# A hybrid decoder block with a product-key expert mixer: which token blocks are gathered, which are multiplied densely, and what runs on GpSimd

## The chip, the core and the metric

The kernel runs on one core of one Trainium2 chip. The metric is the device time of one execution in microseconds (us). Engines are named as in the profile: PE (TensorE matmuls), DVE (VectorE), ACT (ScalarE), POOL (GpSimd), SP (SyncE, which here only issues DMAs).

## The reference

The input is one sequence of 1024 tokens with 1024 features, in float32. After two attention-like mixers and a residual, each token goes through a mixer of 16384 single-neuron experts. Cut to what the change touches:

```
h2 = modulate(x, norm2_g, shift2, scale2)
q  = h2 @ w_q                                # 8 heads x 256
s1, s2 = q halves against 128 keys each      # 8 heads
# top 16 of each, then top 16 of the 256 sums -> 8*16 = 128 experts per token
experts = e1 * 128 + e2 ;  gates = softmax(scores)
a   = gelu(<h2[t], u_tab[experts[t, e]]>)    # 128 dot products of 1024 per token
out = sum_e gates[t, e] * a[t, e] * v_tab[experts[t, e]]
x   = rms_norm(x + gate2 * out, final_g)
```

## The kernel before, in words

The tokens stand in 8 blocks of 128. A **prelude** is run for each group of four blocks (512 tokens): norm, projections, gated linear attention, window attention, second norm, and the choice of the 128 experts of each token. Then comes the expert mixer, which is done in one of two ways.

**Gathered blocks** (blocks 0, 6 and 7). For each of the 128 chosen slots j, POOL issues an indirect DMA that fetches for each of the 128 tokens its own row of `peer_u` (a tile `u` of 128x1024, 512 KB; L605). DVE multiplies it with the tokens' rows `h2s` and sums (L610, which also leaves a short read of the accumulator). Every eighth slot is multiplied on POOL instead (L607) and summed on ACT (L608). When all 128 sums of a block are there, they go through gelu, and 128 rows of `peer_v` are gathered in the same way (L623) and added up with their weights on DVE (L625, tile `yacc`). All gathered tiles share six buffers of the pool `gp` (tag "g"), and so does `h2l`, the load from which PE transposes a gathered block's rows into `h2s`: a gather waits until the multiply that uses its buffer's last tile is done.

**Dense blocks** (blocks 1 to 5, DT = 640 tokens). All 16384 experts are multiplied, as 128 tiles of 128 experts, and the gates of experts that were not chosen are zero. Float32 matmuls are made of three passes each (L165 to L167) on tiles split in a high and a low part (ACT makes the high part, DVE subtracts: `uh` L696, `vl` L723, `wl` L718).
- `dense_u`: the tile's product with the 640 tokens, in two halves of 320 columns (8 x 3 matmuls each), then gelu into `ga`.
- `build_gates`: for each four tokens, two one-hot tiles (`o1` 4 x 128x128 on DVE L671; `o2` 128x512 on POOL L661 and ACT, one of four on DVE L659) go through PE (L672) and give the gates as a table, which is stored to DRAM (`gd`).
- `dense_w`: `gl = gd * ga` on POOL (L715), then its split `wl`.
- `dense_v`: for groups of VG = 3 tiles, 10 outputs of 128x512 (5 blocks x 2 halves) get 3 x 3 matmuls each. Three outputs stay in PSUM throughout (`keep`); the other seven are added to `acc` in SBUF on DVE (L741).

While the gates are built (no `dense_w` can run yet), 60 of the 128 tiles have their first product done ahead (`AHEAD`), 12 of them before the gates begin (`N1`). Their `ga` goes to DRAM (`gad`, issued by POOL) and comes back later. The dense blocks' transposed tokens `h2T` are loaded from DRAM after the second prelude (`load_h2T`).

The order of the instructions on each engine is decided when the program is built, by a scheduler that follows the code's priorities; on the chip each engine takes its instructions strictly in that order. The first 72 slots (`NU`) of block 0 are written before `build_gates`, its others and its `peer_v` rows after the first `o1`.

Of the kernel before, what the change touches and what calls it, by code (L numbers as in the profile page):

```python
# [41 lines left out]
def hymba_peer_kernel(ctx, tc, x, c, w_adaT, b_adaT, g1T, g2T, w_in, w_alpha, b_alphaT,  # L42
# [545 lines left out]
    def token_rows(blk, pool):  # L588
        g, b = divmod(blk, GB)
        h2 = gp.tile([128, 8, 128], F, name="h2l", tag="g")  # L590
        GP.dma_start(h2, h2d[g][:, :, b * 128:b * 128 + 128].rearrange("k p t -> p k t"))
# [6 lines left out]
        return h2s, sm.tile([128, 128], F, name="acts", tag="acts", bufs=1)  # L598

    def gather_u(blk, sel, work, j0=0, j1=128):  # L600
        exi, gates = sel
# [11 lines left out]
        wg = sm.tile([128, 128], F, name="wts", tag="wts", bufs=2)
        A.activation(wg, a, AF.Gelu)
        V.tensor_tensor(wg, wg, gates, AL.mult)
        return wg
# [32 lines left out]
    def build_gates(lists):  # L649
        """gd[b][i2][i1][t] = the sum of the gates of token t for expert (i1, i2)"""  # L650
        for b in range(ND):
            st = gt.tile([128, 128, 128], F, name="st", tag="st", bufs=1)
            for t0 in range(0, 128, 4):
# [4 lines left out]
                if t0 % 16 == 0:  # L658
                    V.tensor_tensor(o2, bc(iota.unsqueeze(1), [128, 4, 128]), e2, AL.is_equal)  # L659
                else:  # L660
                    GP.tensor_tensor(o2, bc(iota.unsqueeze(1), [128, 4, 128]), e2, AL.subtract)  # L661
                    A.activation(o2, o2, AF.Abs)
                    A.activation(o2, o2, AF.Relu, bias=1.0, scale=-1.0)
                for t in range(4):
                    e1, gate = (lists[:, n, b, t0 + t:t0 + t + 1] for n in (0, 2))
                    if t == 3 and t0 % 16 == 0:
                        A.activation(o1[:, t], iota, AF.Abs, bias=e1, scale=-1.0)
                        A.activation(o1[:, t], o1[:, t], AF.Relu, bias=1.0, scale=-1.0)
                        A.activation(o1[:, t], o1[:, t], AF.Copy, scale=gate)
                    else:  # L670
                        first.append(V.tensor_scalar(out=o1[:, t], in0=iota, scalar1=e1, scalar2=gate, op0=AL.is_equal, op1=AL.mult))  # L671
# [8 lines left out]
    def load_h2T():  # L680
        h2T = hx.tile([128, 2, 8, DT], R, name="h2T", tag="hT")
        n0 = GT - D0 * 128
        for k in range(8):
            raw = h2T[:, 1, k].bitcast(F)
            SP.dma_start(raw[:, :n0], h2d[0][k][:, D0 * 128:])
            SP.dma_start(raw[:, n0:], h2d[1][k][:, :DT - n0])
            A.activation(h2T[:, 0, k], raw, AF.Copy)
            GP.tensor_tensor(h2T[:, 1, k], raw, h2T[:, 0, k], AL.subtract)
        return h2T
# [186 lines left out]
```

## Time and profile before

| what | value |
|---|---|
| median of three runs | 3136.61 us (3133.43 to 3137.14) |
| span of the profiled execution | 3135.7 us, 0.9 us under that median |
| PE busy | 2808.3 us (90%) |
| DVE busy | 2747.9 us (88%) |
| POOL busy | 1982.1 us (63%) |
| ACT busy | 1169.0 us (37%) |
| moved by DMA | 767.16 MB, of these 427.61 MB issued by POOL |

Busy is the time in which an instruction of the engine runs, including the time that an instruction needs longer because another engine holds what it needs. Waiting is not busy. The shares are averages over stages that differ much, so the span is looked at in stages below.

### The profile page before, as it was taken

How to read it: one execution, taken by the hardware profiler on the slowest of the kernel's cores; microseconds unless marked ns; L12 is line 12 of the kernel's file. 1: busy time of each engine (PE TensorE's matmuls, PEld its weight loads, DVE VectorE, ACT ScalarE, POOL GpSimd, SP SyncE). 2: the span in 40 equal slices, each digit the busy share in tenths (PEclk: the TensorE clock that was granted, in tenths of full speed). 3: DMA queues.
4: the chain of work that ended last, by engine and by line, in shares of the span. 5: the costliest groups of instructions: out<-in, count | busy, mean ns of one | idle time of the engine just before them, and what ended most of it. 6: DMA issues, size and time to landing. Idle time of an engine off the chain costs nothing. (4 is left out here: it accounts for less than half of the span.)

```text
span 3135.7 us, 45458 instructions
## 1 busy us (share of the span) xinstructions
PE 2808.3 (90%) x15951; PEld 2487.2 (79%) x15951; DVE 2747.9 (88%) x4922; ACT 1169.0 (37%) x2181; POOL 1982.1 (63%) x1679
## 2 busy tenths in 40 slices
PE   5899978888888888888887999999999999999997
PEld 4698766767778877878787888888888887888886
DVE  7754699996599998898895899999999898999998
ACT  4444633343523454565462322222222322322222
POOL 2322565885454775554554688787777788877774
PEclk8999989967999999999998999999999999999998
DMA  8404312565522576757759899999999898999995
GB/s 315 164 29 132 124 55 96 196 224 168 169 68 95 191 244 251 285 184 295 267 193 378 291 309 318 323 311 342 345 334 339 289 333 306 322 317 333 335 333 182
DMA packets 296677, 767.16 MB, mean 245 GB/s; under 512 B 26992, under 2 KB 115328, under 8 KB 293888
## 3 DMA queue, kind: packets, MB, share of 16 engines
q0 software_dynamic: 116832, 427.61, 39.2%
q1 hardware_dynamic: 176736, 294.70, 27.7%
q10 hardware_dynamic: 2880, 41.94, 3.3%
q8 instruction: 125, 2.05, 0.3%
q14 instruction: 104, 0.85, 0.1%
HBM read 689.96 MB, written 74.71 MB: 244 GB/s over the span
## 5 line engine op out<-in xcount | busy, mean ns | idle before, releaser
L623 POOL DMA_INDIRECT v<-in_peer_v_dram,exi x384 | 523.2, 1363 | 354.9 <-DVE yacc L625 183.9
L167 PE MATMUL da<-h2T,uh 128*128 128x320 f32 x2048 | 649.1, 317 | 43.7 <-DVE uh L696 43.7
L165 PE MATMUL da<-h2T,uh 128*128 128x320 f32 x2048 | 649.5, 317 | 13.7 <-ACT ga L702 7.8
L605 POOL DMA_INDIRECT u<-in_peer_u_dram,exi x384 | 546.2, 1422 | 169.3 <-DVE acts L610 71.8
L166 PE MATMUL da<-h2T,uh 128*128 128x320 f32 x2048 | 647.0, 316 | 0.0
L625 DVE SCALAR_TENSOR_TENSOR yacc<-v,wts,yacc 128x1024 f32<-128x1024 f32 x381 | 537.3, 1410 | 29.1 <-DMA v<-in_peer_v_dram,exi 25.1
L610 DVE CUSTOM_DVE_ANT_0 u<-u,h2s 128x1024 f32<-128x1024 f32 x336 | 497.1, 1500 | 20.8 <-DMA u<-in_peer_u_dram,exi 19.2
L167 PEld LDWEIGHTS da<-h2T,uh 128*128 128x128 f32 x2048 | 395.9, 193 | 58.0 <-DVE uh L696 48.7
L165 PEld LDWEIGHTS da<-h2T,uh 128*128 128x128 f32 x2048 | 396.8, 194 | 26.6 <-ACT ga L702 10.4
L166 PEld LDWEIGHTS da<-h2T,uh 128*128 128x128 f32 x2048 | 396.4, 194 | 9.7
L165 PE MATMUL dv<-vl,wl 128*128 128x512 f32 x896 | 358.1, 400 | 29.3 <-DVE acc L741 25.1
L166 PE MATMUL dv<-vl,wl 128*128 128x512 f32 x896 | 352.9, 394 | 0.2 <-DVE vl L723 0.2
L167 PE MATMUL dv<-vl,wl 128*128 128x512 f32 x896 | 352.8, 394 | 0.0
L671 DVE TENSOR_SCALAR o<-iota,lists 128x128 f32<-128x128 f32 x600 | 320.7, 603 | 5.6 <-PE gt L672 5.6
L702 ACT ACTIVATE ga<-da 128x320 f32<-128x320 f32 x256 | 108.7, 430 | 467.9 <-PE da L167 374.5
L157 POOL TENSOR_TENSOR whl<-wraw,whl 128x512 fp32r<-128x512 f32 x104 | 147.1, 1419 | 209.5 <-ACT whl L156 199.3
L672 PE MATMUL gt<-o,o 128*128 128x128 f32 x1280 | 183.8, 291 | 68.6 <-DVE o L671 37.7
L715 POOL TENSOR_TENSOR gl<-gl,ga 128x640 f32<-128x640 f32 x128 | 218.0, 1704 | 23.7 <-issue 12.2
L672 PEld LDWEIGHTS gt<-o,o 128*128 128x128 f32 x1280 | 166.6, 200 | 83.6 <-DVE o L671 36.2
L696 DVE TENSOR_TENSOR uh<-ur,uh 128x1024 fp32r<-128x1024 f32 x128 | 185.2, 1447 | 45.1 <-ACT uh L695 45.0
L165 PEld LDWEIGHTS dv<-vl,wl 128*128 128x128 f32 x896 | 169.3, 189 | 68.7 <-DVE acc L741 35.3
L717 ACT ACTIVATE wl<-gl 128x640 fp32r<-128x640 f32 x128 | 94.3, 737 | 339.6 <-POOL gl L715 222.4
(264 smaller groups left out, 6176.7 us busy)
## 6 DMA issues: line engine op xcount, KB each, us to landing
ur<-in_peer_uT_dram SPq DMA_DIRECT2D x128, 512.0 KB, 6.3
vr<-in_peer_v_dram SPq DMA_DIRECT2D x128, 512.0 KB, 6.9
gd<-st ACTq DMA_DIRECT2D x20, 2048.0 KB, 19.9
gl<-gd SPq DMA_DIRECT2D x128, 320.0 KB, 7.0
wada<-in_w_adaT_dram SPq DMA_DIRECT2D x48, 512.0 KB, 5.4
wraw<-in_w_in_dram SPq DMA_DIRECT2D x80, 256.0 KB, 3.0
gad<-ga POOLq DMA_DIRECT2D x60, 320.0 KB, 4.8
ga<-gad SPq DMA_DIRECT2D x60, 320.0 KB, 4.7
```

The costliest lines, as they stand in the source:

```text
L157: (GP if kq % 2 or (not busy[0] and src is w_q) else V).tensor_tensor(hl[:, 1], raw, hl[:, 0], AL.subtract)
L165: PE.matmul(p, lhsT=lh[0], rhs=rh[0], start=first, stop=False)
L166: PE.matmul(p, lhsT=lh[0], rhs=rh[1], start=False, stop=False)
L167: PE.matmul(p, lhsT=lh[1], rhs=rh[0], start=False, stop=last)
L605: GP.indirect_dma_start(out=u, out_offset=None, in_=peer_u, in_offset=bass.IndirectOffsetOnAxis(ap=exi[:, j:j + 1], axis=0))
L610: V.tensor_tensor_reduce(out=u, in0=u, in1=h2s, scale=1.0, scalar=0.0, op0=AL.mult, op1=AL.add, accum_out=a[:, j:j + 1])
L623: GP.indirect_dma_start(out=v, out_offset=None, in_=peer_v, in_offset=bass.IndirectOffsetOnAxis(ap=exi[:, j:j + 1], axis=0))
L625: V.scalar_tensor_tensor(out=y, in0=v, scalar=wg[:, j:j + 1], in1=y, op0=AL.mult, op1=AL.add)
L671: first.append(V.tensor_scalar(out=o1[:, t], in0=iota, scalar1=e1, scalar2=gate, op0=AL.is_equal, op1=AL.mult))
L672: PE.matmul(p[:, t * 128:t * 128 + 128], lhsT=o2[:, t], rhs=o1[:, t], start=True, stop=True)
L696: V.tensor_tensor(hl[:, 1], u, hl[:, 0], AL.subtract)
L715: GP.tensor_tensor(g, g, ga, AL.mult)
```

## The change

- Blocks 0 to 3 (the first prelude's group) are gathered, blocks 4 to 7 (the second prelude's) are dense: DT goes from 640 to 512, one matmul of 512 columns in place of two of 320, 8 dense outputs in place of 10 (5 in `acc` in place of 7). There are 512 `u` and 512 `v` gathers in place of 384 and 384.
- `h2T` stays in SBUF from the second prelude; `load_h2T` is gone.
- All `u` multiplies are on DVE (L606 of the changed kernel), as are `gl = gd * ga` (L694) and all `o1` (L661). Half of the `o2` are on DVE (L654) and half on ACT alone (L657, L658). POOL keeps the gathers and the preludes' work.
- 40 tiles are done ahead in place of 60, 4 of them before the gates; the DMA that stores `ga` is issued by ACT.
- All `u` gathers of blocks 0 to 2 are written before `build_gates`, those of block 3 after the ahead tiles; all `v` gathers come after, with the dense tiles.

```diff
-D0 = 1
-ND = 5
+D0 = 4
+ND = 4
...
-    NU = 72
+    NU = 3
...
-            if j % 8 == 7:
-                GP.tensor_tensor(u, u, h2s, AL.mult)
-                A.activation(u, u, AF.Copy, accum_out=a[:, j:j + 1])
-            else:
-                V.tensor_tensor_reduce(out=u, in0=u, in1=h2s, scale=1.0, scalar=0.0, op0=AL.mult, op1=AL.add, accum_out=a[:, j:j + 1])
+            V.tensor_tensor_reduce(out=u, in0=u, in1=h2s, scale=1.0, scalar=0.0, op0=AL.mult, op1=AL.add, accum_out=a[:, j:j + 1])
...
-                if t0 % 16 == 0:
+                if t0 % 8 == 0:
                     V.tensor_tensor(o2, bc(iota.unsqueeze(1), [128, 4, 128]), e2, AL.is_equal)
                 else:
-                    GP.tensor_tensor(o2, bc(iota.unsqueeze(1), [128, 4, 128]), e2, AL.subtract)
-                    A.activation(o2, o2, AF.Abs)
+                    for t in range(4):
+                        A.activation(o2[:, t], iota, AF.Abs, bias=lists[:, 1, b, t0 + t:t0 + t + 1], scale=-1.0)
                     A.activation(o2, o2, AF.Relu, bias=1.0, scale=-1.0)
...
-        GP.tensor_tensor(g, g, ga, AL.mult)
+        V.tensor_tensor(g, g, ga, AL.mult)
...
-    N1 = 12
-    NX = 46
-    ORDER = (0, 7, 1, 2, 8, 3, 4, 9, 5, 6)
-    AHEAD = {i: n for n, i in enumerate(range(1, 120, 2))}
+    N1 = 4
+    ORDER = (0, 5, 1, 2, 6, 3, 4, 7)
+    AHEAD = {i: n for n, i in enumerate(range(1, 120, 3))}
...
-            GP.dma_start(gad[AHEAD[i]], ga)
+            A.dma_start(gad[AHEAD[i]], ga)
...
-        with tc.high_priority(offset=600):
-            h2T = load_h2T()
         for i in tiles[:N1]:
             ahead(i)
         decode(GB, NB)
-        gather_u(0, sels[0], work0, 0, NU)
+        wgs = [gather_u(0, sels[0], work0)]
+        for b in range(1, NU):
+            wgs.append(gather_u(b, sels[b], token_rows(b, sm)))
...
         build_gates(lists)
-        with tc.issue_after(first[0].ins):
-            y0 = gather_v(0, sels[0], gather_u(0, sels[0], work0, NU), sm)
         for n, i in enumerate(tiles[N1:]):
-            ahead(i, ux if n < NX and n % 2 == 1 else None)
+            ahead(i, ux if n % 2 == 1 else None)
+        with tc.issue_after(first[0].ins):
+            for b in range(NU, D0):
+                wgs.append(gather_u(b, sels[b], token_rows(b, sm)))
...
-    finish([y0], 0, GP)
-    for b in range(D0 + ND, NB):
-        finish([gather_v(b, sels[b], gather_u(b, sels[b], token_rows(b, sm)), sm)], b, GP)
+    for b in range(D0):
+        finish([gather_v(b, sels[b], wgs[b], sm)], b, GP)
```

Three places of the built order are needed below. The first is POOL. Before, its last work in the second prelude reads as follows (`whl` is a weight split of the prelude, `swr`, `grr` and `e` are small work of its norms and attention, xN counts equal rows):

```order
L605 DMA u<-in_peer_u_dram,exi 128x1024 x5
L305 TENSOR_TENSOR e<-e,kg 128x512
L605 DMA u<-in_peer_u_dram,exi 128x1024 x2
L607 TENSOR_TENSOR u<-u,h2s 128x1024
L605 DMA u<-in_peer_u_dram,exi 128x1024 x8
L607 TENSOR_TENSOR u<-u,h2s 128x1024
L605 DMA u<-in_peer_u_dram,exi 128x1024 x3
L147 TENSOR_TENSOR swr<-swv,mhalf 128x1
```

In the changed kernel the same stretch reads as follows (`h2l`, L591, is the load of the rows of the next gathered block, here block 1):

```order
L605 DMA u<-in_peer_u_dram,exi 128x1024 x5
L305 TENSOR_TENSOR e<-e,kg 128x512
L605 DMA u<-in_peer_u_dram,exi 128x1024 x19
L147 TENSOR_TENSOR swr<-swv,mhalf 128x1
L605 DMA u<-in_peer_u_dram,exi 128x1024 x24
L147 TENSOR_TENSOR swr<-swv,mhalf 128x1
L605 DMA u<-in_peer_u_dram,exi 128x1024
L445 TENSOR_TENSOR grr<-gss,mhalf 128x4
L605 DMA u<-in_peer_u_dram,exi 128x1024 x3
L591 DMA h2l<-h2d 128x8x128
```

More gathers stand ahead of the prelude's small work: over the whole second prelude 133 (block 0 and five of block 1) in place of 72, and no L607 in place of nine. After the prelude POOL's order is this, with only the small work of three finishes between the `v` gathers that follow:

```order
L605 DMA u<-in_peer_u_dram,exi 128x1024 x123
L591 DMA h2l<-h2d 128x8x128
L605 DMA u<-in_peer_u_dram,exi 128x1024 x128
L591 DMA h2l<-h2d 128x8x128
L605 DMA u<-in_peer_u_dram,exi 128x1024 x128
L618 DMA v<-in_peer_v_dram,exi 128x1024 x128
```

The `h2l` of block 2 stands behind the last 123 gathers of block 1.

The second place is PE, where the gates begin (`gt` is their PSUM tile, `dl` the transposes of the last expert lists, `h2p` the transposes of a gathered block's rows, `da` an ahead tile). Before:

```order
L165 MATMUL da<-h2T,uh 128x320
L672 MATMUL gt<-o_10167,o_10168 128x128 x3
L166 MATMUL da<-h2T,uh 128x320
L672 MATMUL gt<-o_10167,o_10168 128x128
L167 MATMUL da<-h2T,uh 128x320
```

Changed:

```order
L596 MATMUL h2p<-ident,h2l 128x128 x8
L584 MATMUL dl<-ident,ee 128x128
L584 MATMUL dl<-ident,gates 128x128
L596 MATMUL h2p<-ident,h2l 128x128 x8
L662 MATMUL gt<-o_10487,o_10488 128x128 x4
L662 MATMUL gt<-o_10500,o_10501 128x128 x4
L165 MATMUL da<-h2T,uh 128x512
```

The first eight `h2p` are those of block 1, the second eight those of block 2; the second now stand ahead of the first gate matmul and of 36 ahead tiles. On DVE the 123 multiplies of block 1 stand at the same place, with only 16 `o1` and 2 `o2` ahead of most of them.

The third place is the end of DVE's order. Before, the last `v` multiply stood between the last dense work:

```order
L741 TENSOR_TENSOR acc<-dv,acc 128x512
L625 SCALAR_TENSOR_TENSOR yacc<-v,wts,yacc 128x1024
L636 TENSOR_TENSOR yl<-yacc,rows 128x1024
L637 TENSOR_TENSOR x1l<-x1l,yl 128x1024
L741 TENSOR_TENSOR acc<-dv,acc 128x512
L718 TENSOR_TENSOR wl<-gl,wl 128x640
```

Changed:

```order
L720 TENSOR_TENSOR acc<-dv,acc 128x512
L620 SCALAR_TENSOR_TENSOR yacc<-v,gates,yacc 128x1024
L720 TENSOR_TENSOR acc<-dv,acc 128x512
L620 SCALAR_TENSOR_TENSOR yacc<-v,gates,yacc 128x1024 x117
L631 TENSOR_TENSOR yl<-yacc,rows 128x1024
L631 TENSOR_TENSOR yl<-acc,rows 128x512 x4
```

117 `v` multiplies of block 3 now stand behind the last `acc`, and the dense blocks' own finishes (`yl<-acc`) behind them.

## Rows read from the trace of the kernel before

**Rows 1.** Windows (us): length; busy of PE, PEld, DVE, ACT, POOL; PEclk; DMA share; GB/s.

```profile
537.00:742.00 205.00, 168.59 (x976) 144.42 (x974) 186.92 (x330) 76.04 (x177) 173.33 (x119) 0.76 0.68 223
742.00:1042.00 300.00, 262.64 (x1603) 235.23 (x1604) 241.28 (x1008) 120.41 (x255) 135.75 (x229) 0.95 0.32 106
1042.00:1700.00 658.00, 553.53 (x3699) 533.50 (x3698) 584.94 (x891) 345.10 (x690) 382.48 (x337) 0.94 0.72 256
1700.00:3090.00 1390.00, 1348.77 (x6929) 1174.53 (x6928) 1313.15 (x1342) 372.71 (x533) 1072.22 (x698) 0.99 0.92 322
3090.00:3136.00 46.00, 24.02 (x119) 19.99 (x117) 32.55 (x39) 10.17 (x17) 13.81 (x11) 0.81 0.28 104
2100.00:2300.00 200.00, 197.96 (x1018) 172.71 (x1017) 192.90 (x182) 50.80 (x72) 157.04 (x103) 1.00 0.96 338
```

**Rows 2.** POOL's groups by line: count | busy us, mean ns | idle before, and releasers.

```profile
L605 POOL DMA_INDIRECT u<-in_peer_u_dram,exi x384 | 546.2, 1422 | 169.3 <-DVE acts L610 71.8 <-issue 63.7 <-DVE o L671 11.5
L623 POOL DMA_INDIRECT v<-in_peer_v_dram,exi x384 | 523.2, 1363 | 354.9 <-DVE yacc L625 183.9 <-DVE o L671 82.5 <-issue 44.6
L715 POOL TENSOR_TENSOR gl<-gl,ga 128x640 f32<-128x640 f32 x128 | 218.0, 1704 | 23.7 <-issue 12.2 <-DVE vl L723 7.3 <-DMA gl<-gd 2.2
...
L661 POOL TENSOR_TENSOR o<-iota,lists 128x512 f32<-128x512 f32 x120 | 137.5, 1156 | 24.4 <-PE gt L672 22.5
L607 POOL TENSOR_TENSOR u<-u,h2s 128x1024 f32<-128x1024 f32 x48 | 120.7, 2514 | 1.3 <-DMA u<-in_peer_u_dram,exi 0.5
```

**Rows 3.** DVE's groups by line, same columns.

```profile
L625 DVE SCALAR_TENSOR_TENSOR yacc<-v,wts,yacc 128x1024 f32<-128x1024 f32 x381 | 537.3, 1410 | 29.1 <-DMA v<-in_peer_v_dram,exi 25.1
L610 DVE CUSTOM_DVE_ANT_0 u<-u,h2s 128x1024 f32<-128x1024 f32 x336 | 497.1, 1500 | 20.8 <-DMA u<-in_peer_u_dram,exi 19.2 <-DVE acc L741 1.0 <-ACT h2s L597 0.4
L671 DVE TENSOR_SCALAR o<-iota,lists 128x128 f32<-128x128 f32 x600 | 320.7, 603 | 5.6 <-PE gt L672 5.6
L741 DVE TENSOR_TENSOR acc<-dv,acc 128x512 f32<-128x512 f32 x294 | 197.0, 681 | 5.1 <-PE dv L167 5.0
L723 DVE TENSOR_TENSOR vl<-vr,vl 128x1024 fp32r<-128x1024 f32 x128 | 188.4, 1476 | 14.1 <-ACT vl L722 14.0
```

**Rows 4.** Timeline of DVE while the gates are built: start, duration, instruction.

```profile
1400.72 3.61 DVE L671 TENSOR_SCALAR o<-iota,lists 128x128 f32<-128x128 f32 x4
1404.25 1.21 DVE L696 TENSOR_TENSOR uh<-ur,uh 128x1024 fp32r<-128x1024 f32 x1
1405.38 1.27 DVE L625 SCALAR_TENSOR_TENSOR yacc<-v,wts,yacc 128x1024 f32<-128x1024 f32 x1
...
1411.79 0.34 DVE L671 TENSOR_SCALAR o<-iota,lists 128x128 f32<-128x128 f32 x1
```

**Rows 5.** Timeline of POOL in the same stretch.

```profile
1402.20 2.04 POOL L661 TENSOR_TENSOR o<-iota,lists 128x512 f32<-128x512 f32 x2
```

**Rows 6.** Timeline of PE in the dense stage.

```profile
2235.61 0.39 PE L165 MATMUL dv<-vl,wl 128*128 128x512 f32 x1
...
2237.43 0.39 PE L167 MATMUL dv<-vl,wl 128*128 128x512 f32 x1
2237.65 0.30 PE L165 MATMUL da<-h2T,uh 128*128 128x320 f32 x1
...
2238.38 0.31 PE L167 MATMUL da<-h2T,uh 128*128 128x320 f32 x1
```

**Rows 7.** Timeline of POOL in the second prelude, idle time and releaser in brackets.

```profile
700.52 0.94 POOL L605 DMA_INDIRECT u<-in_peer_u_dram,exi  x1 [0.30 <-issue]
701.76 0.94 POOL L605 DMA_INDIRECT u<-in_peer_u_dram,exi  x1 [0.30 <-issue]
703.00 1.70 POOL L605 DMA_INDIRECT u<-in_peer_u_dram,exi  x1 [0.30 <-issue]
705.01 1.69 POOL L605 DMA_INDIRECT u<-in_peer_u_dram,exi  x1 [0.30 <-DVE mx L343]
```

**Rows 8.** Timeline of DVE in the same stretch.

```profile
702.66 1.23 DVE L610 CUSTOM_DVE_ANT_0 u<-u,h2s 128x1024 f32<-128x1024 f32 x1
```

More of the change, by code (lines that the diff above doesn't have):

```diff
@@ L65, in hymba_peer_kernel @@
     x1d = [dp.tile([128, D], F, name=f"x1d{b}", tag=f"x1d{b}") for b in range(NB)]
-    h2d = [dp.tile([8, 128, GT], F, name=f"h2d{g}", tag=f"h2d{g}") for g in range(NG)]
+    h2d = dp.tile([8, 128, GT], F, name="h2d", tag="h2d")
     badaT = cst("badaT", [128, 48])
@@ L482, in prelude @@
         for k in range(8):
-            transpose_split([ys[b][:, k * 128:(k + 1) * 128] for b in range(GB)], h2T, k, A2[:, k:k + 1], modT[:, 24 + k:25 + k], h2d[g][k])
+            transpose_split([ys[b][:, k * 128:(k + 1) * 128] for b in range(GB)], h2T, k, A2[:, k:k + 1], modT[:, 24 + k:25 + k], None if g else h2d[k])
         if g == 0:
@@ L510, in prelude @@
         res[g] = sels
+        h2Ts[g] = h2T
     def top16(s, v, i, n):
@@ L588, in token_rows @@
     def token_rows(blk, pool):
-        g, b = divmod(blk, GB)
         h2 = gp.tile([128, 8, 128], F, name="h2l", tag="g")
-        GP.dma_start(h2, h2d[g][:, :, b * 128:b * 128 + 128].rearrange("k p t -> p k t"))
+        GP.dma_start(h2, h2d[:, :, blk * 128:blk * 128 + 128].rearrange("k p t -> p k t"))
         h2s = pool.tile([128, D], F, name="h2s", tag="h2s", bufs=1)
@@ L597, in token_rows @@
             A.activation(h2s[:, hf * 512:hf * 512 + 512], h2p, AF.Copy)
-        return h2s, sm.tile([128, 128], F, name="acts", tag="acts", bufs=1)
+        return h2s, sm.tile([128, 128], F, name="acts", tag="acts", bufs=2)
     def gather_u(blk, sel, work, j0=0, j1=128):
@@ L605, in gather_u @@
             GP.indirect_dma_start(out=u, out_offset=None, in_=peer_u, in_offset=bass.IndirectOffsetOnAxis(ap=exi[:, j:j + 1], axis=0))
-            if j % 8 == 7:
-                GP.tensor_tensor(u, u, h2s, AL.mult)
-                A.activation(u, u, AF.Copy, accum_out=a[:, j:j + 1])
-            else:
-                V.tensor_tensor_reduce(out=u, in0=u, in1=h2s, scale=1.0, scalar=0.0, op0=AL.mult, op1=AL.add, accum_out=a[:, j:j + 1])
+            V.tensor_tensor_reduce(out=u, in0=u, in1=h2s, scale=1.0, scalar=0.0, op0=AL.mult, op1=AL.add, accum_out=a[:, j:j + 1])
         if j1 < 128:
             return
[L613 to L616, printed above, removed]
+        A.activation(a, a, AF.Gelu)
+        V.tensor_tensor(gates, a, gates, AL.mult)
+        return gates
     def gather_v(blk, sel, wg, pool):
@@ L665, in build_gates @@
                     e1, gate = (lists[:, n, b, t0 + t:t0 + t + 1] for n in (0, 2))
[L666 to L671, printed above, removed]
+                    first.append(V.tensor_scalar(out=o1[:, t], in0=iota, scalar1=e1, scalar2=gate, op0=AL.is_equal, op1=AL.mult))
                     PE.matmul(p[:, t * 128:t * 128 + 128], lhsT=o2[:, t], rhs=o1[:, t], start=True, stop=True)
@@ L678, in hymba_peer_kernel @@
     HALF = [(i * DT // 2, DT // 2) for i in range(2)] if DT > 512 else [(0, DT)]
[L680 to L689, printed above, removed]
     def dense_u(i, h2T, pool=None):
@@ L779, in hymba_peer_kernel @@
         qkv.close()
-        hx = ctx.enter_context(tc.tile_pool(name="hd", bufs=1, side="right", reuse_waits="tile"))
+        h2T = h2Ts[1]
         du = ctx.enter_context(tc.tile_pool(name="du", bufs=2, side="right", reuse_waits="tile"))
@@ L798, in hymba_peer_kernel @@
         build_gates(lists)
+        for n, i in enumerate(tiles[N1:]):
+            ahead(i, ux if n % 2 == 1 else None)
         with tc.issue_after(first[0].ins):
-            y0 = gather_v(0, sels[0], gather_u(0, sels[0], work0, NU), sm)
-        for n, i in enumerate(tiles[N1:]):
-            ahead(i, ux if n < NX and n % 2 == 1 else None)
+            for b in range(NU, D0):
+                wgs.append(gather_u(b, sels[b], token_rows(b, sm)))
     dv = ctx.enter_context(tc.tile_pool(name="dv", bufs=1, reuse_waits="tile"))
```

4 lines of the change are left out of this document (2 added, 2 removed).

## The prediction

> **What bounds the kernel now.** I read the windows first, since the average shares (PE 90%, DVE 88%) hide the stages. [rows 1] has five stages from the second prelude's first gather (537 us) on. In 537 to 742 POOL is busy 173 of 205 us and DVE 187: gathers and the prelude share POOL's queue. In 742 to 1042 the choice of experts and the first ahead tiles run, with PE at 263 of 300 us. In 1042 to 1700, while the gates are built, DVE is the fullest with 585 of 658 us (89%). In 1700 to 3090 the dense tiles run: PE 1349 of 1390 us (97%), DVE 1313, DMA share 0.92. The last 46 us finish. So PE bounds the long stage, with DVE and DMA close behind; what a change is worth there is read from PE.
>
> Second, the lines of DVE and the timelines, for how much of DVE's busy time is its own. A one-hot `o1` takes 0.34 us when POOL is idle and 3.61/4 = 0.90 while POOL's L661 runs [rows 4, 5]. The mean over all 600 is 0.603 [rows 3]. So 600 x (0.603 - 0.34) = 158 us of this line are waiting for POOL. The same for `u` (mean 1.50 against 1.23 [rows 8]) is 336 x 0.27 = 91 us, for `yacc` (1.41 against 1.27) 53 us, for `vl` (1.476 against the 1.21 of `uh`, which has its shape) 34 us, and for `uh` about as much. Together some 370 us of DVE's 2748.
>
> Third, the steps in which engines can go. Consecutive DVE instructions overlap by 0.08 us (1404.25 + 1.21 against 1405.38), so a `yacc` costs 1.19 us of DVE, `uh` or `vl` 1.13, `o1` 0.26, a 128x512 `acc` 0.60, and a `u` with its read 1.23 [rows 3, 4, 8]. Nine 512-column matmuls start within 1.82 us, 0.2275 each; six of 320 columns within 0.73 us, 0.146 each [rows 6].
>
> **What the change does to the totals.** PE: a tile's first product goes from 48 x 0.146 = 7.0 to 24 x 0.2275 = 5.46 us, its second from 30 x 0.2275 = 6.83 to 5.46: 128 x 2.91 = 372 us less. DVE: the stretch of some 370 us goes, and what comes is 176 `u` x 1.23 = 216, 128 `yacc` x 1.19 = 152, 128 `gl` x 0.60 = 77, less 84 `acc` = 50: +395 against -370, so DVE stays at about 2750 us. DMA: 256 more gathers of 0.524 MB (+134 MB) against smaller `gl`, `ga`, `gd`. PE's saving counts only where PE is the bound, so I go by stages.
>
> **Second prelude and choice of experts (before: to 1042).** POOL issues 133 gathers in place of 72, ahead of the small norm work for which the prelude waits. POOL had 173 of 205 us plus 0.30 us of issue between gathers, so it was full. A gather's mean is 1.42 us [rows 2], with the 0.30 gap 1.72: 61 x 1.7 = 104 us more, less nine L607 of 2.51 = 23: +81. DVE alone would ask for 65 more multiplies x 1.23 = 80, less its 18 us of slack: +62. Eight ahead tiles fewer take 62 us of PE out of the next window, where DVE has 241 of 300 us; of that I count -12, bounds 0 and -40. Sum **+69** (30 to 100): 1111 us.
>
> **Block 1's gathers alone.** PE's transposes of block 2's rows (`h2p`) now stand ahead of the first gate matmul, and their `h2l` stands on POOL behind 123 gathers of block 1. In that time PE, and behind it ACT's evictions and the stored tables, have nothing to do: before, PE was busy 84% in the same part. The step of a gather alone is not in the trace. From below: 1.24 us, POOL's free step (700.52 to 701.76 [rows 7]). From above: 2.01 (703.00 to 705.01). By DMA: 0.524 MB at 338 GB/s, the rate at share 0.96 [rows 1], is 1.55. By DVE 1.23. I take 1.6, nearest to the DMA row and between it and the mean 1.72. 123 x 1.6 + 8 for the `h2l` and the transposes = **205 us** (160 to 255).
>
> **Gates (before: 658 us).** The built order leaves 190 `u` (234 us), 496 `o1` (129), 62 `o2` (37) and 40 `uh` (45) to DVE: 445 us. PE needs less: 36 ahead tiles x 5.46 = 197 and four fifths of the gate matmuls, in a stage where it was busy 554 with 48 longer tiles and all of them. With DVE at its 89% of before, 445/0.89 = **500 us** (450 to 540).
>
> **Dense tiles (before: 1390 us).** PE: 82 first and 128 second products, 210 x 5.46 = 1147. DVE: 66 `u`, 395 `yacc`, 210 `acc`, 126 `gl`, 127 `wl`, 127 `vl`, 82 `uh` = 1066. DMA: 461 gathers, 124 `vr`, 82 `ur` of 0.524 MB and some 43 MB of `gl` and `ga`, 393 MB; at 338 GB/s 1163. At PE's 97% of before it would be 1182. Three needs now lie within 100 us and `gl` stands in DVE's order, so I take **1200 us** (1150 to 1250): 190 less than before, of which fewer `yacc` in this stage are a part, since the rest comes next.
>
> **The tail.** 117 `v` multiplies of block 3 stand behind the last `acc`, and the dense blocks' finishes behind them; PE has no work. 117 x 1.6 = 187, and 24 for the last finishes, about half of the old 46 us, in which dense work still ran [rows 1]: **211 us** (165 to 260).
>
> Sum: 1111 + 205 + 500 + 1200 + 211 = 3227, against 3135.7 of the span; the median stands 0.9 above it, so **3230 us**. The moves that I cost at nothing: `load_h2T` and its eight POOL subtracts go, hidden under the prelude; the `ga` stores and half of the `o2` (four Abs and a Relu each) come to ACT, which was busy 345 of 658 us in the gates and now has four blocks' tables to evict in place of five. Should ACT fill up there, its excess over 500 us is added.
>
> **A rule that speaks for a smaller price.** In the two lone stretches a gather starts, as a buffer comes free, just when the next multiply starts. Started at 703.00, 0.34 us into a `u` multiply, it took 1.70 us, started as DVE did other work 0.94 [rows 7, 8]: the multiply holds it.
>
> The Trainium skill (SBUF — State Buffer, "Who interferes with whom") says that a DVE instruction with two SBUF inputs contends only with GpSimd work that reads SBUF, and infers that a `tensor_tensor` doesn't hold descriptor generation, which needs the write interface. By that rule the step alone would be POOL's free 1.24 and the two stretches 240 x 0.36 = 86 us shorter, 3144. The row of 1.70 speaks against it for this multiply.
>
> **Rivals.**
>
> *Dense and gate stages at the engines' own pace (faster).* With POOL out of DVE's way the 11% that DVE lost in the gates and the 3% of PE may vanish: gates 445, dense tiles 1147, together 108 less: 3120. It decides once the two stages stay under some 1608 us. For it: the 370 us of stretch came in bursts (single instructions of 0.90 in place of 0.34) that delayed PE. Against it: DMA would have to move 393 MB in 1147 us, 343 GB/s, above the best window. Chance 0.18.
>
> *Unheld gathers.* The lone stretches go at 1.24, POOL's free step: 3144. Against it: that is 423 GB/s, and no window moves more than 338; at DMA's 1.55 only 12 us are won. Chance 0.09.
>
> *The second prelude hides the added gathers.* If the norm work was not waiting for POOL, 61 gathers cost nothing: 3230 - 69 = 3161. For it: PE has 36 us idle of 205, so nothing is quite full. Against: POOL with its gaps is. Chance 0.08.
>
> *Every lone gather held.* Step 2.01 in both stretches, + 0.4 x 240 = 96 us: 3326. For it: the two rows of 1.70 and 1.69 in succession. Against it: while a gather is held its multiply can't come, and DVE runs dry. Chance 0.13.
>
> **How the numbers follow.** My forecast has 0.52, with 3160 to 3300 for itself. Leaving out the outer parts of the first and the last rival gives 3105 to 3325. A measurement of this kernel tells about 0.2% (6 us) from no change. Faster: the first rival, and a little of the unheld gathers: 0.2. Same: 0.06. Slower: 0.74.
>
> **What would show it.** First `o1` wave at about 1110 us; then some 200 us in which PE stands nearly still and DVE shows only `u`; a second such stretch of `yacc` alone at the end; DVE's mean for `o1` near 0.34 and for `yacc` near 1.27. The prediction is wrong if the gathers of the lone stretches step at 1.3 us or less, if PE works in them, or if the gate and dense stages together come under 1610 us.

## The result, and the profile after

The changed kernel takes 3172.86 us (median of four runs, 3166.45 to 3177.29) against 3136.88 us before (four runs). The ratio is 1.0113, 95% interval 1.0095 to 1.0131: slower by 36 us. The profiled execution has a span of 3174.9 us. Two of the variants below had one run each at a lower granted clock, 13% and 24% longer, and their medians are of the other three.

Busy times and three of the 40-slice rows of the page after (each digit is the busy share of a slice in tenths, PEclk the granted clock):

```profile
PE 2397.1 (76%) x11860; PEld 2001.5 (63%) x11860; DVE 2728.7 (86%) x5385; ACT 997.1 (31%) x1871; POOL 1756.6 (55%) x1573
...
PE   5899978776898000659789499999999999999400
...
PEclk8999989865799555759899799999999999999755
DMA  8413313788531299998987999999999999999997
```

PE has lost 411 us of busy time, and DVE has kept its own (2728.7 against 2747.9). PE's row shows two holes, at a third of the span and at the end. DMA's row is full from the first hole to the end.

The same stretch in windows (columns as in [rows 1]); the first `o1` starts at 1093 us, the first gate matmul at 1284, the first `gl` at 1797, the last `acc` at 2971, the last `yacc` at 3143:

```profile
742.00:1093.00 351.00, 246.58 (x1291) 207.51 (x1290) 289.26 (x1106) 106.89 (x247) 175.76 (x255) 0.77 0.38 128
1093.00:1283.00 190.00, 0.49 (x3) 0.52 (x4) 157.41 (x266) 0.79 (x2) 150.40 (x126) 0.50 0.95 343
1283.00:1797.00 514.00, 387.61 (x1999) 329.16 (x1997) 430.76 (x980) 242.20 (x521) 278.09 (x193) 0.82 0.90 325
1797.00:2971.00 1174.00, 1168.28 (x5088) 955.25 (x5088) 1096.05 (x1216) 333.81 (x436) 631.59 (x469) 1.00 0.95 338
2971.00:3144.00 173.00, 0.00 (x0) 0.00 (x0) 150.35 (x118) 0.00 (x0) 131.07 (x114) 0.50 0.97 353
3144.00:3174.90 30.90, 0.00 (x0) 0.00 (x0) 18.76 (x23) 5.62 (x10) 11.24 (x8) 0.50 0.36 135
...
1093.00:3144.00 2051.00, 1556.38 (x7088) 1284.93 (x7088) 1834.57 (x2578) 576.80 (x959) 1191.15 (x900) 0.87 0.94 337
```

The five terms of the sum can be read off. The second hole and the first are the forecast's two lone stretches: 0.00 and 0.49 us of PE, with DVE on one kind of multiply. In both, DMA is at 0.95 to 0.97 and 343 to 353 GB/s, more than in the best window of [rows 1] (338). In the dense stage PE is busy 99.5%. Over the whole of the last row, DMA share 0.94 stands against PE 76%: before, the dense stage had 0.92 against 97%.

The hole in PE's timeline, with the idle time and its releaser in brackets:

```profile
1086.51 0.42 PE L584 MATMUL dl<-ident,gates 128*128 128x128 f32 x1
1282.51 1.94 PE L596 MATMUL h2p<-ident,h2l 128*128 128x128 f32 x8 [195.58 <-DMA h2l<-h2d]
1284.24 2.13 PE L662 MATMUL gt<-o,o 128*128 128x128 f32 x9
```

POOL issued that load at 1275.76, behind the 123 gathers of block 1:

```profile
1275.76 0.97 POOL L591 DMA_DIRECT2D h2l<-h2d  x1
```

That is the wait which the built order showed: block 2's transposes hold the gate matmuls until `h2l` has come behind block 1's gathers.

DVE's groups after, for comparison with [rows 3]:

```profile
L620 DVE SCALAR_TENSOR_TENSOR yacc<-v,gates,yacc 128x1024 f32<-128x1024 f32 x508 | 650.7, 1281 | 26.4 <-DMA v<-in_peer_v_dram,exi 18.7 <-DVE yacc L620 0.5
L606 DVE CUSTOM_DVE_ANT_0 u<-u,h2s 128x1024 f32<-128x1024 f32 x512 | 631.7, 1249 | 85.0 <-DMA u<-in_peer_u_dram,exi 77.3 <-ACT h2s L597 3.4 <-DVE acts L606 0.4
...
L661 DVE TENSOR_SCALAR o<-iota,lists 128x128 f32<-128x128 f32 x512 | 147.0, 359 | 0.0
```

With POOL's elementwise work gone, the means fall to about what single unhindered instructions took before: `yacc` 1.41 to 1.28, `u` 1.50 to 1.25, `o1` 0.603 to 0.359.

### The profile page after: what moved, and what is told of

Its sections match the earlier page's. It is cut to its first block, busy times and chain, and to the rows that moved or that the text cites. A ratio compares the mean times of both kernels' runs of the same rounds, so it can differ in the third digit from the quotient of the medians.

```text
span 3174.9 us, 37296 instructions
## 1 busy us (share of the span) xinstructions
PE 2397.1 (76%) x11860; PEld 2001.5 (63%) x11860; DVE 2728.7 (86%) x5385; ACT 997.1 (31%) x1871; POOL 1756.6 (55%) x1573
## 2 busy tenths in 40 slices
DMA packets 311318, 861.55 MB, mean 271 GB/s; under 512 B 30016, under 2 KB 99920, under 8 KB 309072
## 5 line engine op out<-in xcount | busy, mean ns | idle before, releaser
L618 POOL DMA_INDIRECT v<-in_peer_v_dram,exi x512 | 677.1, 1323 | 498.2 <-DVE yacc L620 399.0
L605 POOL DMA_INDIRECT u<-in_peer_u_dram,exi x512 | 688.6, 1345 | 393.7 <-DVE acts L606 247.1
L606 DVE CUSTOM_DVE_ANT_0 u<-u,h2s 128x1024 f32<-128x1024 f32 x512 | 631.7, 1249 | 85.0 <-DMA u<-in_peer_u_dram,exi 77.3
L620 DVE SCALAR_TENSOR_TENSOR yacc<-v,gates,yacc 128x1024 f32<-128x1024 f32 x508 | 650.7, 1281 | 26.4 <-DMA v<-in_peer_v_dram,exi 18.7
L165 PE MATMUL da<-h2T,uh 128*128 128x512 f32 x1024 | 406.9, 397 | 44.6 <-ACT ga L681 43.5
L167 PE MATMUL da<-h2T,uh 128*128 128x512 f32 x1024 | 407.2, 398 | 42.9 <-DVE uh L675 42.9
L166 PE MATMUL da<-h2T,uh 128*128 128x512 f32 x1024 | 403.5, 394 | 0.0
L165 PE MATMUL dv<-vl,wl 128*128 128x512 f32 x640 | 251.1, 392 | 1.2 <-DVE acc L720 1.0
L167 PE MATMUL dv<-vl,wl 128*128 128x512 f32 x640 | 250.0, 391 | 0.0
L166 PE MATMUL dv<-vl,wl 128*128 128x512 f32 x640 | 249.9, 391 | 0.0
L167 PEld LDWEIGHTS da<-h2T,uh 128*128 128x128 f32 x1024 | 194.5, 190 | 87.5 <-DVE uh L675 45.9
L165 PEld LDWEIGHTS da<-h2T,uh 128*128 128x128 f32 x1024 | 194.9, 190 | 86.4 <-ACT ga L681 44.8
L166 PEld LDWEIGHTS da<-h2T,uh 128*128 128x128 f32 x1024 | 194.7, 190 | 41.9
L674 ACT ACTIVATE uh<-ur 128x1024 fp32r<-128x1024 f32 x128 | 135.2, 1057 | 244.3 <-issue 158.9
L720 DVE TENSOR_TENSOR acc<-dv,acc 128x512 f32<-128x512 f32 x210 | 143.3, 687 | 37.2 <-PE dv L167 36.8
L702 DVE TENSOR_TENSOR vl<-vr,vl 128x1024 fp32r<-128x1024 f32 x128 | 156.0, 1219 | 1.7 <-ACT vl L701 1.6
```

Source lines behind the costliest of these rows:

```text
L165: PE.matmul(p, lhsT=lh[0], rhs=rh[0], start=first, stop=False)
L166: PE.matmul(p, lhsT=lh[0], rhs=rh[1], start=False, stop=False)
L167: PE.matmul(p, lhsT=lh[1], rhs=rh[0], start=False, stop=last)
L618: GP.indirect_dma_start(out=v, out_offset=None, in_=peer_v, in_offset=bass.IndirectOffsetOnAxis(ap=exi[:, j:j + 1], axis=0))
L620: V.scalar_tensor_tensor(out=y, in0=v, scalar=wg[:, j:j + 1], in1=y, op0=AL.mult, op1=AL.add)
L702: V.tensor_tensor(vl[:, 1], v, vl[:, 0], AL.subtract)
```

## The experiments

Two theories were set against each other. **Idle PE:** the changed kernel loses the time in which PE stands still, 190 and 173 us. **DMA:** the gathers that the fourth gathered block adds (861.55 MB moved in place of 767.16) fill the DMA engines from the first `o1` to the end, so that it matters little where PE stands still. Beside that, the change was taken apart.

**One block's gathers ahead of the gates in place of three.**

```diff
-    NU = 3
+    NU = 1
```

> The changed kernel with only block 0's u gathers written before the gates (blocks 1 to 3 after the first o1). In the built order no h2p stands ahead of the first gate matmul any more, 87 u multiplies lie among the gates' o1 in place of 297, and 325 v multiplies stand behind the last acc in place of 117. Idle PE is the loss: the stretch of 190 us without PE goes and nothing comes in its place, about 2985 us. DMA is the bound (share 0.95 to 0.97 from the first o1 on): the stretch goes, the gates get shorter, and the tail grows by 208 gathers at 1.47 us = 306, so about 3176 us, within 1% of the changed kernel.

Measured: 3237.09 us (ratio to before 1.0334, 1.0298 to 1.0369), slower than the changed kernel by 64 us. Its windows:

```profile
1078.00:1529.00 451.00, 367.34 (x2014) 316.57 (x2014) 340.60 (x825) 248.47 (x538) 144.54 (x102) 0.90 0.74 270
1529.00:2697.00 1168.00, 1163.82 (x5082) 950.74 (x5081) 1078.57 (x1428) 331.02 (x433) 639.02 (x473) 1.00 0.95 341
2697.00:3193.00 496.00, 0.53 (x3) 0.10 (x1) 426.08 (x337) 2.30 (x4) 380.85 (x329) 0.50 0.96 348
1078.00:3193.00 2115.00, 1531.69 (x7096) 1267.41 (x7095) 1845.25 (x2587) 581.79 (x975) 1164.42 (x903) 0.86 0.91 327
```

The hole is gone and the gates take 451 us in place of 190 + 514. All of it, and more, comes back as a tail of 496 us: PE stands idle for 583 of these 2115 us, against 495 of 2051 in the changed kernel, so the hole was moved and not removed. The forecast of the idle-PE theory (2985) falls; that of the DMA theory (3176) was 61 us too low. DMA's busy time from the first `o1` to the last `yacc` is the same in both: 2115 x 0.91 = 1925 us here, 2051 x 0.94 = 1928 us in the changed kernel. By itself that shows little, since both move the same 861.5 MB; what differs is how full DMA was. It was at 0.74 while the gates were built, and that is what my expectation of 3176 missed.

**All four blocks' `u` gathers ahead of the gates.**

```diff
-    NU = 3
+    NU = 4
```

> The changed kernel with all four blocks' u gathers written before the gates. In the built order PE's transposes of blocks 2 and 3 both stand ahead of the first gate matmul, behind 251 gathers in place of 123, and 1 v multiply stands behind the last acc in place of 117. If an idle PE is what a lone stretch costs, it depends on the order only by what moves: 128 gathers more ahead of the gates (+196 us) and 116 fewer in the tail (-170), and fewer among the gates: 3165 to 3190 us. If filling DMA early gives back what the later stages lack, as three blocks ahead were 64 us better than one: 3100 to 3150.

Measured: 3187.29 us (1.0158, 1.013 to 1.0187).

```profile
1084.00:1465.00 381.00, 4.03 (x18) 3.69 (x19) 315.08 (x523) 2.97 (x7) 297.88 (x255) 0.50 0.96 351
1465.00:1975.00 510.00, 388.62 (x2004) 330.99 (x2003) 423.57 (x910) 245.69 (x523) 243.25 (x177) 0.82 0.88 316
1975.00:3148.00 1173.00, 1162.64 (x5069) 950.21 (x5067) 1098.38 (x1146) 329.89 (x430) 631.69 (x469) 1.00 0.95 338
1084.00:3148.00 2064.00, 1555.29 (x7088) 1284.89 (x7088) 1837.03 (x2578) 578.55 (x959) 1172.82 (x900) 0.86 0.93 335
```

PE's hole is twice as long (381 us), the tail is gone, and the kernel takes 14 us more than the changed one. It came as the first reading had it (3165 to 3190); the second, that filling DMA early gives time back (3100 to 3150), fell. From the first `o1` on DMA's share was 0.94 with three blocks ahead and is 0.93 with four, so there was nothing left to fill. Three orders, from no hole with a long tail to a long hole with no tail, have one DMA time (here 2064 x 0.93 = 1920 us), as their equal bytes let one expect, and their stretch from the first `o1` to the last `yacc` exceeds it by 123 to 190 us.

**Every second `vr` load left out.**

```diff
+        if i % 2 == 0:
+            vr[0] = dv.tile([128, D], F, name="vr", tag="vr", bufs=2)
+            SP.dma_start(vr[0], peer_v[i * 128:i * 128 + 128, :])
+        v = vr[0]
```

> The changed kernel in which every odd expert tile uses the peer_v rows of the tile before it, so 64 loads of vr (33.5 MB) are left out; all instructions of PE, DVE, ACT and POOL stay. If DMA bounds the dense stage, 33.5 MB at 343 GB/s = 98 us less, about 3075 us. If PE bounds it (1168 of 1174 us busy), no gain there: 3160 to 3175 us, with a dense stage of about 1170 us at a DMA share near 0.87.

Measured: 3234.66 us (1.0306, 1.0277 to 1.0335), slower, with a dense stage of 1232 us at DMA share 0.87. Neither theory expected that.

**Half the columns of each `vr` load left out.**

```diff
-        SP.dma_start(v, peer_v[i * 128:i * 128 + 128, :])
+        SP.dma_start(v[:, :512], peer_v[i * 128:i * 128 + 128, :512])
...
+        vv = bc(v[:, :512].unsqueeze(1), [128, 2, 512])
```

> The changed kernel with 512 of the 1024 columns of each vr tile loaded, used twice (33.5 MB of peer_v left out); every instruction of PE, DVE, ACT and POOL keeps its size and SP its order, so that no load comes later, as gl did when every second vr was left out. DMA bounds the dense stage: 98 us less, about 3075 us. PE bounds it: the dense stage stays 1165 to 1180 us at a DMA share near 0.86, and the kernel 3160 to 3180 us.

Measured: 3275.08 us (1.0437, 1.042 to 1.0455), slower still. Three of its longest waits in the dense stage (waiter, awaited: total us, times, longest):

```profile
ACT vl L703 <- DMA vr<-in_peer_v_dram: 250.0, 40, 10.6
ACT ga L681 <- DVE gl L694: 239.1, 31, 9.2
DVE gl L694 <- DMA gl<-gd: 156.4, 67, 6.6
```

DVE waits 156 us at `gl` for its load; in the changed kernel it is 11.6 us in all. With smaller loads the scheduler built another order on SP and DVE (112 `v` multiplies in the tail in place of 117, `gl` and `vr` loads in another sequence), in which `gl` and `vr` stand too close to their loads, and DVE's whole queue waits behind them. That the scheduler reckons with a shorter load than the chip needs is how I read it; it wasn't tried. My expectation that SP keeps its order was wrong. Both experiments changed two things, so they say nothing about DMA against PE in the dense stage, and the windows show both nearly full there (PE 99.5%, DMA 0.95). They do show that with fewer bytes and no work added another built order went with 62 and 102 us more.

**The elementwise work off POOL, alone,** in the kernel before.

```diff
-            if j % 8 == 7:
-                GP.tensor_tensor(u, u, h2s, AL.mult)
...
-                if t0 % 16 == 0:
+                if t0 % 8 == 0:
...
-                    GP.tensor_tensor(o2, bc(iota.unsqueeze(1), [128, 4, 128]), e2, AL.subtract)
...
-        GP.tensor_tensor(g, g, ga, AL.mult)
+        V.tensor_tensor(g, g, ga, AL.mult)
```

> The kernel before with one part of the change alone: the elementwise work of the expert mixer off POOL (u and gl multiplies on DVE, o2 half on DVE and half on ACT, all o1 on DVE); blocks and bytes as before. If POOL's stretch of DVE (some 370 us) held PE up: gates 658 to about 570 us, dense stage 1390 to about 1350 (PE's 1343 at 99.5%), so 3010 to 3060 us. If that stretch was off the path: 3125 to 3145. If DVE becomes the bound with what it takes over: above 3145.

Measured: 3008.92 us (0.9595, 0.957 to 0.962), 127 us faster than before and the fastest of all versions here. Windows of before and of this variant, gates and dense stage (from the first `o1` to the first second product, and from there to the last one):

```profile
1042.00:1704.00 662.00, 556.84 (x3720) 536.55 (x3719) 585.70 (x892) 346.96 (x693) 383.80 (x337) 0.94 0.72 257
1704.00:3115.00 1411.00, 1369.41 (x7024) 1191.47 (x7024) 1329.46 (x1361) 376.43 (x539) 1078.27 (x702) 0.99 0.91 317
```

```profile
1042.00:1603.00 561.00, 512.35 (x3662) 507.13 (x3660) 445.33 (x971) 317.10 (x719) 221.53 (x192) 0.96 0.79 289
1603.00:2984.00 1381.00, 1361.17 (x7070) 1193.59 (x7071) 1263.60 (x1568) 340.40 (x475) 764.33 (x561) 1.00 0.93 330
```

The gates are 101 us shorter, the dense stage 30 us. In the gates DVE's busy time falls from 586 to 445 us though it has taken over work. The `o1` alone, all in this stage, fall from 320.7 us for 600 ([rows 3]) to 178.0 us for 640:

```profile
L662 DVE TENSOR_SCALAR o<-iota,lists 128x128 f32<-128x128 f32 x640 | 178.0, 353 | 1.2 <-PE gt L663 1.2
```

**Its two halves.** With `u`, `o1` and `o2` off POOL and `gl` left there, and with `gl` alone moved:

> The kernel before with the u multiplies, o1 and o2 off POOL and gl left on POOL; the same order on DVE as the variant with all of it off POOL (3009 us), but for gl. If the gain of that variant came from the gate stage, where o1 waited for POOL: 3010 to 3035 us, with gates of about 560 us. If it came from gl's stretch of the dense stage: 3090 to 3110.

> The kernel before with gl alone moved from POOL to DVE. If the gate stage holds the gain: 3115 to 3140 us, the dense stage at most 20 us shorter. If gl's stretch held PE up in the dense stage: 3090 to 3110, the dense stage near 1350 us.

Measured: 3014.93 us (0.961, 0.959 to 0.963) and 3101.17 us (0.9881, 0.9861 to 0.9901). The first has gates of 564 and a dense stage of 1387 us, the second 669 and 1367. So most of the gain lies in the gates, where `o1` is no longer held by POOL's work (120 `o2` and seven `u` multiplies there). `gl` alone gives 39 us (44 in the dense stage, less 7 in the gates), but once the rest is off POOL only 6, which is no more than the kernel before differs between the two sessions (3135.62 and 3140.52). The first came as the gate theory had it; the second came as its rival had it, though with a dense stage of 1367 and not 1350. Each half works in its own stage, and together they give less than their sum.

**`gl` back on POOL in the changed kernel.**

```diff
-        V.tensor_tensor(g, g, ga, AL.mult)
+        GP.tensor_tensor(g, g, ga, AL.mult)
```

> The changed kernel with gl = gd * ga back on POOL, all else as it is. If keeping POOL out of DVE's way is what lets PE run at 99.5% in the dense stage (1168 of 1174 us), that stage goes back to PE's 97% of before, 1205 to 1215 us, and the kernel to 3200 to 3220 us. If POOL's stretch is off the path: 3165 to 3180. If DVE's load is what counts, its 88 us fewer let PE start earlier and v multiplies leave the tail: about 3150.

Measured: 3184.26 us (1.0151, 1.0134 to 1.0168), 11 us slower than the changed kernel, between the first expectation and the second. Its dense stage has PE at 99.3% with POOL's `gl` in it:

```profile
1800.00:2975.00 1175.00, 1167.08 (x5081) 955.66 (x5080) 1134.61 (x1084) 330.75 (x431) 856.42 (x594) 1.00 0.95 335
```

So `gl`'s place is not why PE runs at 99.5% there. No run isolates what is: with POOL freed, four dense blocks and 60 tiles done ahead (the second variant of the next experiment) PE was busy 1085 of 1112 us, 97.5%, with DMA at 0.96.

**Four dense blocks, alone,** in the kernel before, and then with the elementwise work off POOL too.

```diff
-ND = 5
+ND = 4
...
-    ORDER = (0, 7, 1, 2, 8, 3, 4, 9, 5, 6)
+    ORDER = (0, 5, 1, 2, 6, 3, 4, 7)
```

> The kernel before with four dense blocks in place of five (1 to 4; 0, 5, 6 and 7 gathered), DT 512 and the order of 8 outputs; POOL's elementwise work as before. The built order leaves 112 u and 252 v multiplies behind the last acc. Bytes bound it: the tail alone costs 364 x 1.47 = 535 us, and the dense stage ends some 300 us sooner for PE's saving, so 3200 to 3260 us, slower than both. If PE's saving of 372 us counted: 2800 to 2900 us.

> The kernel before with two parts of the change, the elementwise work off POOL and four dense blocks (1 to 4) in place of five; its way of loading h2T, its 60 ahead tiles and its 72 u gathers under the second prelude stay. In the built order 128 u and 254 v multiplies stand behind the last acc. Stage by stage: 1042 + 500 + 1130 + 382 x 1.48 = 565 + 31 give 3270 us. If the two parts simply add (309 us more and 127 less): 3318. If the u gathers under the prelude bring nothing, it ends level with the changed kernel, 3173.

Measured: 3444.68 us (1.0989, 1.0958 to 1.102) alone, 215 us above my expectation's middle, and 3237.32 us (1.033) together with the other part, 33 below it. Of the 215 us, the expectation's own terms (300 us sooner, a tail of 535) explain most: they add up to about 3370, not to 3200 to 3260. Alone, the tail takes 630 us for some 380 gathers (the 112 `u` and 252 `v` multiplies on DVE, and 16 `u` multiplied on POOL), 1.66 each: those 16 multiplies take 38 us of POOL, and a `u` gather 1.37 us of it. With POOL freed a `u` gather takes 1.17 us, and 382 gathers 568 us, 1.49 each:

```profile
2640.00:3208.00 568.00, 2.20 (x8) 1.43 (x8) 484.50 (x514) 2.65 (x5) 439.47 (x381) 0.50 0.96 353
```

The two parts don't add: off POOL is worth 127 us with five dense blocks and 207 with four.

**72 of block 0's 128 `u` gathers under the second prelude,** in the variant with one block ahead.

```diff
-        wgs = [gather_u(0, sels[0], work0)]
+        gather_u(0, sels[0], work0, 0, 72)
...
+            wgs.append(gather_u(0, sels[0], work0, 72))
```

> The variant with one block's u gathers ahead of the gates, with 72 of its 128 ahead and 56 after the first o1. If the gathers prolong the second prelude by POOL (1.7 us each less POOL's slack), the first o1 comes at 1042 to 1050 in place of 1078 us. The 56 gathers come back as some 33 among the gates and 19 more in the tail (28 us), so the kernel as a whole stays within 20 us of that variant's 3237. If the prelude hides gathers: first o1 still at 1075 to 1080, the kernel 3260.

Measured: 3243.69 us (1.0333, 1.0316 to 1.0351), 7 us above that variant, which its runs (3225 to 3251 us) do not tell apart. The first `o1` comes at 1032 us in place of 1078: 56 gathers prolong the second prelude by 46 us, 0.82 us each. Put off, they come back later in full.

**All 128 of them under the prelude,** with the elementwise work off POOL and five dense blocks.

```diff
-        gather_u(0, sels[0], work0, 0, NU)
+        wg0 = gather_u(0, sels[0], work0)
```

> The kernel before with the elementwise work off POOL (3009 us) and a second part of the change: all 128 u gathers of block 0 under the second prelude in place of 72. If the 56 gathers prolong that prelude where it isn't bound by DMA, the first o1 comes at 1085 to 1095 in place of 1042 us; 30 v gathers come out of the dense stage, where PE is the bound and gains nothing, so 3035 to 3055 us. If gathers done early pay wherever they stand, as they did for the changed kernel: 2990 to 3010.

Measured: 3037.41 us (0.9677, 0.9654 to 0.9701), 28 us slower than without. The first `o1` comes at 1090 in place of 1042. Here, where PE is the fullest (99% of the dense stage), gathers done early cost. In the changed kernel three blocks ahead were 64 us better than one, but neither 56 gathers of block 0 (7 us) nor a fourth block (14 us the other way) gained anything, so that early gathers pay wherever DMA is the bound is not shown.

## Why the prediction was wrong

The sign and the stages came out; the size did not: +36 us in place of +93. By its own terms, from the windows after:

| term | forecast | measured |
|---|---|---|
| to the first `o1` | 1111 | 1093 |
| block 1's gathers alone | 205 | 190 |
| gates | 500 | 514 |
| dense tiles | 1200 | 1174 |
| tail and finishes | 211 | 204 |

Four terms of five were too high, by 18, 15, 26 and 7 us, and one too low, by 14: together 52 us. Since the change is the small difference of large gains and losses, these 52 us are more than half of the forecast effect.

**The dense term was the largest miss.** The step that failed is "Three needs now lie within 100 us and `gl` stands in DVE's order, so I take 1200". PE's 97% of before alone gave 1182, 8 above the measured 1174; the 18 us on top rested on no row, and they did not come: PE was busy 99.5% (1168 us), beside DMA at 0.95 and DVE at 93%. The first rival, stages at the engines' own pace, was right in kind here, but its 1147 was as far too low as my 1200 was too high: the stage held 5088 matmuls where I had counted 210 x 24 = 5040, at 0.230 us each in place of 0.2275. The argument against it, that DMA would have to move 343 GB/s, was borne out: DMA moved 338 through the whole stage, just what it had in the best window of [rows 1] (one stretch of 100 us, 2100 to 2200, had 340).

**The gates** came 14 us longer than forecast, though DVE had 14 us less to do (431 in place of 445): DVE was busy 84% of the stage, not the 89% of before that I divided by. The first rival's 445 us was further off. What held DVE there I have not separated.

**The second prelude** was priced by POOL: 61 x 1.7 less nine L607 = +81, less 12. By the prelude's last `grr` on POOL (756 us before, 819 after) the gathers cost +62; from there to the first `o1` it is 286 and 274 us, the forecast's -12. So the 81 was 19 too high, and the forecast's price by DVE (+62) is the one that came out, by its number. Taking the nine L607 off moved the first `o1` by less than 1 us (1042 in both), since POOL then waited for DVE. Its last `swr` of the prelude, in the variant with that work off POOL and 72 gathers, and in the changed kernel with 133:

```profile
745.74 0.55 POOL L147 TENSOR_TENSOR swr<-swv,mhalf 128x1 f32<-128x1 f32 x1 [24.82 <-DVE swv L145]
```

```profile
797.02 0.98 POOL L147 TENSOR_TENSOR swr<-swv,mhalf 128x1 f32<-128x1 f32 x1
```

So part of the added gathers filled a gap of POOL's. Each of 56 cost 0.82 us there on average (the split variant) or 48/56 = 0.86 (the last variant). With 133 gathers both queues are nearly full (from 537 to 797 us POOL with 218 us of work and 24 between gathers, DVE with 244); which of them sets that price I have not separated.

**The lone gathers.** I took 1.6 us, between 1.55 for DMA and the mean 1.72. The first stretch needs 190/123 = 1.54, the tail 173/117 = 1.48: near DMA's pace. POOL's and DVE's groups in the first stretch:

```profile
L605 POOL DMA_INDIRECT u<-in_peer_u_dram,exi x125 | 150.6, 1204 | 39.9 <-issue 35.6 <-DVE acts L606 3.0 <-DVE o L661 1.2
```

```profile
L606 DVE CUSTOM_DVE_ANT_0 u<-u,h2s 128x1024 f32<-128x1024 f32 x123 | 150.3, 1225 | 31.6 <-DMA u<-in_peer_u_dram,exi 28.4 <-DVE acts L606 0.4
```

The claim that "the multiply holds it" was right, and single instructions of this stretch show how long:

```profile
1153.55 1.65 POOL L605 DMA_INDIRECT u<-in_peer_u_dram,exi  x1 [0.31 <-issue]
1155.51 1.28 POOL L605 DMA_INDIRECT u<-in_peer_u_dram,exi  x1 [0.30 <-issue]
1157.09 0.95 POOL L605 DMA_INDIRECT u<-in_peer_u_dram,exi  x1 [0.30 <-issue]
```

```profile
1153.15 1.23 DVE L606 CUSTOM_DVE_ANT_0 u<-u,h2s 128x1024 f32<-128x1024 f32 x1 [0.72 <-DMA u<-in_peer_u_dram,exi]
...
1154.74 1.23 DVE L606 CUSTOM_DVE_ANT_0 u<-u,h2s 128x1024 f32<-128x1024 f32 x1 [0.35 <-DMA u<-in_peer_u_dram,exi]
...
1155.98 1.23 DVE L606 CUSTOM_DVE_ANT_0 u<-u,h2s 128x1024 f32<-128x1024 f32 x1
```

Each of the three gathers starts while a multiply runs and ends 0.82 us after that multiply's end (1155.20 against 1154.38, 1156.79 against 1155.97, 1158.04 against 1157.21). Of the 120 gathers that start from 1103.6 to 1283 us, 107 start within a multiply, and all of them end 0.80 to 0.87 us after its end; the other 13 take 0.94 or 0.95 us. What was wrong is the moment at which a gather starts: not as a buffer comes free (POOL waited for that 3.0 us in all), but 0.30 us after the gather before it. 51 of the 107 start in the last quarter microsecond of a multiply and lose at most 0.1 us, so the mean is 1.20 and not 1.70, and neither rival on this (1.24 by POOL's free step, 2.01 with every gather held) came true. The rule of the Trainium skill (SBUF — State Buffer, "Who interferes with whom"), by which such a multiply would not hold a gather's issue at all, is not borne out by these 107 gathers. What set the step of 1.54 I have not separated: DMA was at 0.95, and POOL's queue, with 1.20 us of issue and 0.30 between gathers, was as full (186 of 190 us).

**What was right:** the two stretches without PE, their place and cause; DVE's total (2750 forecast, 2728.7); the fall of `o1`, `u` and `yacc` to about their unhindered durations; and the multiply's hold on a gather. One reading was off: POOL was not idle beside the 0.34 us `o1` but issuing a gather (1411.53 to 1412.69), so that in this row a gather does not lengthen an `o1` as L661 does.

**What was missed in kind:** I saw PE's idle stretches as the loss. In the three orders they move but do not go: from the first `o1` to the last `yacc` PE stands idle for 495, 509 and 583 us. The loss is the fourth gathered block: 256 more gathers, with 94 MB more to move in all (an estimate of 275 us at 343 GB/s). Taken apart, the change is

- elementwise work off POOL: -127 us (3136 to 3009),
- then four dense blocks in place of five: +228 us (3009 to 3237),
- then the rest, the second group as the dense one, `h2T` kept in SBUF, 40 ahead tiles, and three blocks' gathers ahead of the gates: -64 us (3237 to 3173).

In the changed order, going from three blocks ahead back to one costs those same 64 us, so the last item is the early gathers' doing, as far as one edit can tell; that it comes from filling DMA (0.74 against 0.90 in the gates) is how I read it, and a fourth block ahead gave nothing more. The order of the items matters: the first is worth 207 us if it comes second.

Left open: a direct trial of fewer bytes in an unchanged order. That DMA bounds the changed kernel rests on its share (0.94 from the first `o1` to the last `yacc`), not on such a trial; the equal busy time of the three orders (1920 to 1928 us) follows from their equal bytes. A rival stands untested beside it: in the stretches of gathers alone POOL's issuing is as full as DMA, so their price may be POOL's and not the bytes'. And bytes alone do not set the time: the two variants with four dense blocks in the kernel before move 876 MB each and differ by 207 us.

## What to carry to other kernels

A part that takes a slow engine's work off the path can be hidden in a change that loses: try the parts alone before judging the whole. When work moves from a dense product to gathers, price the added gathers over the whole stretch first, by bytes and by issue, then look at who stands idle: here PE's idle time could be moved from a hole to a tail, but no order removed it. And when a change in a scheduler-built kernel makes loads smaller, read the new order before crediting or blaming the bytes.

## What the runs showed of the hardware that was not expected

- Indirect gathers of 512 KB, one after another with six buffers, kept DMA at 0.95 to 0.97 and 343 to 353 GB/s over 173 to 568 us, one gather per 1.48 to 1.54 us. POOL, which issues them, was nearly as full (186 of 190 us in the first stretch).
- A gather that POOL starts while DVE runs a multiply of two 128x1024 tiles was held until that multiply's end: 107 of 107 in the first stretch ended 0.80 to 0.87 us after it, against 0.94 to 0.95 us for a gather started beside none.
- In windows without matmuls the granted clock is shown as 0.50 (1.2 GHz of 2.4), 0.82 in the gates that follow the hole and 1.00 in the dense stage (0.94 in the gates of before). No run here isolates what that costs; DMA was at 0.90 in those gates.
- POOL's elementwise work cost DVE about its own time again: with 138 us of `o2` [rows 2] and 17 us of `u` multiplies off POOL in the gates, DVE's busy time there fell by 140 us though DVE took 40 more `o2` and 40 more `o1`; the `o1` fell from 0.603 to 0.353 us each.
